# Smaller and earlier pieces of x and of the first weights in the opening of a hybrid decoder layer

## The chip, the cores and the metric

One core of one Trainium2 chip runs the whole program. The metric is the device time of one execution in microseconds, so lower is better. A run is repeated and the median is given.

## What is computed

One decoder layer for 256 prompt tokens and 8 sample tokens (264 columns side by side), in three residual sub-layers: attention and a state-space scan in parallel, cross-attention, and a convolutional feed-forward part. The change lies in the very first step, the input projection of the first sub-layer:

```python
def rms_norm(x, g):
    xf = x.astype(jnp.float32)
    y = xf * lax.rsqrt(jnp.mean(xf * xf, axis=-1, keepdims=True) + EPS)
    return (y * g.astype(jnp.float32)).astype(x.dtype)
...
    proj = rms_norm(x, w['g_mix']) @ w['w_in']
    q, k, v, z, xbc, dt_raw = jnp.split(proj, IN_SPLITS, axis=-1)
```

x has 2048 features, that is 16 blocks of 128; `w_in` has 2048 rows and 6688 columns, all in float32.

## The kernel before

Every operand of a product is split into a high part (rounded to a short float) and a low part (the rest), and a product is three matmuls: high weight by high x, high weight by low x, low weight by high x. The gain `g_mix` is multiplied into x while it is split; the norm's reciprocal root is applied after the product. The high parts are written by ScalarE (`x_hi` line 148, `w_hi` line 170), the low parts by VectorE (`x_lo` line 152, `w_lo` line 174); for the first pieces of weights VectorE also writes a high part (line 203).

The opening (lines 186 to 266) is written out by hand: the order in which SyncE, TensorE, ScalarE and VectorE issue their instructions is that of the code. It computes the first 512 columns of the projection in four PSUM banks, `first`, as two pairs p = 0 and 1 of 256 columns each. The loop of line 251 runs over the 16 blocks k of x, and for each block over the two pairs; `first_k` (line 237) issues six matmuls: for one pair, the three products one behind the other, each for two groups m of 128 columns. That is 12 matmuls for a block and 192 in all (line 243 in the trace). They are followed by 16 small float32 products for `dt` (line 249, 32 records in the trace), which multiply x by `wdt`, and by one product that sums the squares of x (line 266). That needs `acc0`, which comes from four squares on ScalarE (line 257) and five sums on VectorE (lines 258 to 263), ordered behind the splits.

Ahead of the first product four float32 matmuls on zeros (line 195) keep TensorE at work while the first data are on the way.

The loads: `load_x(k, n)` (line 142) brings n blocks of x, 132 KB each, by SyncE's queue; `w_load(p, k, n)` (line 160) brings n blocks of pair p, 128 KB each, by SyncE's queue or by ScalarE's. Blocks 0 and 1 come singly, blocks 2 to 7 in pieces of two, blocks 8 to 15 as x in pieces of two and weights in pieces of four. The raw weights of four blocks of a pair share one buffer of the tag `wraw` (line 163), of which there are four, so the raw weights of blocks 8 to 15 take the buffers of blocks 0 to 7 and their transfers are issued once the splits there are done. The high and low weights have four buffers of the same size each (`whi`, `wlo`), and a buffer is free once the products that read it are done.

The tag `B` holds four tiles of 8 by 264 columns. In the opening the two tiles `sw` for the squares take two of them (line 185); `t8`, `cpast`, `kv`, `kcT`, `vc` and `zz` follow. Behind the opening the order of the instructions is that of a planner that goes by modelled times; there `weights` (line 72) loads further weights in parts of 512 KB (line 79) into the same four `wraw` buffers and splits them (lines 85 and 86), and `proj` (line 104) multiplies them. The next pairs of the projection wait in their queues for the sum of line 266 and what goes with it (line 354).

Of the kernel before, what the change touches and what calls it, by code (L numbers as in the profile page):

```python
# [8 lines left out]
F32R = mybir.dt.float32r  # L9
# [6 lines left out]
KB = D // 128  # L16
TP, TS = 256, 8
T = TP + TS
# [29 lines left out]
def hybrid_decoder_step_kernel(ctx: ExitStack, tc: tile.TileContext, I, O):  # L48
    nc = tc.nc
    V, S, P, PE = nc.vector, nc.scalar, nc.gpsimd, nc.tensor  # L50

    cpool = ctx.enter_context(tc.tile_pool(name="cpool", bufs=1))
    wpool = ctx.enter_context(tc.tile_pool(name="wpool", bufs=2))
    apool = ctx.enter_context(tc.tile_pool(name="apool", bufs=1))
# [5 lines left out]
    def psum(tag):  # L60
        return ps.tile([128, 512], F32, tag=tag, name=tag, bufs=banks[tag])

    def T3(pool, n, dt=F32, tag=None, name=None, bufs=None):
        return pool.tile([128, n, T], dt, tag=tag, name=name or tag, bufs=bufs)


    NPART, WBUFS = 1024, 4

    def raw_part(n=NPART):
        return wpool.tile([128, n], F32, tag="wraw", name="wraw", bufs=4)  # L70
# [64 lines left out]
    wdt = T3(apool, 8, F32, "C", "wdt").rearrange("p a t -> p (a t)")[:, 0:512].rearrange("p (k c) -> p k c", c=32)  # L135
    w_in = I["w_in"]
    small = ctx.enter_context(tc.tile_pool(name="small", bufs=2))
    A = []
# [3 lines left out]
    def load_x(k, n):  # L142
        nc.sync.dma_start(out=xT[k // 4][:, k % 4:k % 4 + n, :], in_=I["xT"][:, k:k + n, :])

    def x_of(k):
        return xT[k // 4][:, k % 4, :], par[:, k:k + 1]

    def x_hi(k):
        x, g = x_of(k)
        return S.activation(out=A[k // 8][0][:, k % 8, :], in_=x, func=AF.Copy, scale=g)  # L150

    def x_lo(k):
        x, g = x_of(k)
        return V.scalar_tensor_tensor(out=A[k // 8][1][:, k % 8, :], in0=x, scalar=g, in1=A[k // 8][0][:, k % 8, :].bitcast(F32),
                                      op0=ALU.mult, op1=ALU.subtract)


    pre = {}

    def w_load(p, k, n, on=nc.sync):  # L160

        if k % 4 == 0:
            pre[p, k // 4] = (raw_part(), *(wpool.tile([128, NPART], F32R, tag=t, name=t, bufs=WBUFS) for t in ("whi", "wlo")))
        c = 256 * (k % 4)
        on.dma_start(out=pre[p, k // 4][0][:, c:c + 256 * n], in_=w_in[2 * p + k // 8][:, 256 * (k % 8):256 * (k % 8 + n)])

    def w_piece(p, k, n):
        return (w[:, 256 * (k % 4):256 * (k % 4 + n)] for w in pre[p, k // 4])

    def w_hi(p, k, n):  # L170
        raw, hi, _ = w_piece(p, k, n)
        return S.copy(out=hi, in_=raw)

    def w_lo(p, k, n):
        raw, hi, lo = w_piece(p, k, n)
        return V.tensor_tensor(out=lo, in0=raw, in1=hi.bitcast(F32), op=ALU.subtract)


    acc0 = small.tile([128, T], F32, tag="acc", bufs=1, name="acc0")
    table = small.tile([128, 1], F32, tag="r", bufs=2, name="table")  # L180
    first = [psum(t) for t in ("t", "t", "mm", "s")]
    warm = psum("x")
# [2 lines left out]
    sw = [T3(apool, 8, tag="B", name=f"sw{i}", bufs=4) for i in range(2)]  # L185
    with tc.manual_schedule(engines={mybir.EngineType.SP, mybir.EngineType.PE, mybir.EngineType.Activation, mybir.EngineType.DVE}):
        V.memset(acc0, 0.0)
        load_x(0, 1)
        S.dma_start(out=par[:, 0:16], in_=I["par"][:, 0:16])
        w_load(0, 0, 1, S)  # L190
        w_load(1, 0, 1, S)

        S.activation(out=table, in_=acc0[:, 0:1], func=AF.Copy)
        for _ in range(4):
            PE.matmul(warm[:, :T], acc0[:, 0:128], acc0, start=True, stop=True)
        for k, n in ((1, 1), (2, 2), (4, 2), (6, 2)):
            load_x(k, n)
            for p in range(2):
                w_load(p, k, n)
        for k in (0, 1):  # L200
            x_hi(k)
            raw, hi, _ = w_piece(0, k, 1)
            V.tensor_copy(out=hi, in_=raw)
            w_hi(1, k, 1)
            x_lo(k)
            for p in range(2):
                w_lo(p, k, 1)
        for k in (2, 4, 6):
            x_hi(k)
            w_hi(0, k, 2)  # L210
            w_hi(1, k, 2)
            x_hi(k + 1)
            x_lo(k)
            w_lo(0, k, 2)
            w_lo(1, k, 2)
            x_lo(k + 1)
        for k in (8, 12):
            load_x(k, 2)
            w_load(0, k, 4)
            w_load(1, k, 4)  # L220
            load_x(k + 2, 2)
        nc.sync.dma_start(out=wdt, in_=I["w_dt"])
        for k in (8, 12):
            for i in range(4):
                x_hi(k + i)
                x_lo(k + i)
                if i == 1:
                    w_hi(0, k, 4)
                    w_lo(0, k, 4)
            w_hi(1, k, 4)  # L230
            w_lo(1, k, 4)
        V.tensor_tensor(out=wdt, in0=wdt, in1=par[:, 0:16].unsqueeze(2).broadcast_to([128, KB, 32]), op=ALU.mult)
        nc.sync.dma_start(out=cst, in_=I["cst"])
        nc.sync.dma_start(out=par[:, 16:], in_=I["par"][:, 16:])
        nc.sync.dma_start(out=hcol, in_=I["hcol"])

        def first_k(p, k):
            wh, wl = (w.rearrange("p (k c) -> p k c", c=256)[:, k % 4, :] for w in pre[p, k // 4][1:])
            xh, xl = (a[:, k % 8, :] for a in A[k // 8])

            for i, (w, x) in enumerate(((wh, xh), (wh, xl), (wl, xh))):
                for m in range(2):
                    PE.matmul(first[2 * p + m][:, :T], w[:, m * 128:(m + 1) * 128], x, start=k + i == 0, stop=k == KB - 1 and i == 2)  # L243

        def dt_round(r):

            for j in range(4):
                k = 4 * r + j
                PE.matmul(dt_ps[32 * j:32 * j + 32, :T], wdt[:, k, :], xT[k // 4][:, k % 4, :], start=r == 0, stop=r == 3)

        for k in range(KB):
            for p in range(2):
                first_k(p, k)

        for i in range(2):
            for j in range(2):
                S.activation(out=sw[i][:, 4 * j:4 * j + 4, :], in_=xT[2 * i + j], func=AF.Square)
            V.tensor_tensor(out=sw[i][:, 0:4, :], in0=sw[i][:, 0:4, :], in1=sw[i][:, 4:8, :], op=ALU.add)

        sq_last = S.activation(out=table, in_=sw[1][:, 7, 0:1], func=AF.Sqrt)  # L260
        V.tensor_tensor(out=sw[0][:, 0:4, :], in0=sw[0][:, 0:4, :], in1=sw[1][:, 0:4, :], op=ALU.add)
        V.tensor_tensor(out=sw[0][:, 0:2, :], in0=sw[0][:, 0:2, :], in1=sw[0][:, 2:4, :], op=ALU.add)
        add_last = V.tensor_tensor(out=acc0, in0=sw[0][:, 0, :], in1=sw[0][:, 1, :], op=ALU.add)
        for r in range(4):
            dt_round(r)
        sum_last = PE.matmul(sum0[:, :T], cst[:, C_ONE:C_ONE + 128], acc0, start=True, stop=True)
# [157 lines left out]
    p = psum("y")  # L424
# [38 lines left out]
    p = psum("x")  # L463
# [5 lines left out]
    p = psum("x")  # L469
# [236 lines left out]
    for c in range(2):  # L706
        p = psum("x")
# [4 lines left out]
    for w, XT in enumerate((BT, CT)):  # L712
        p = psum("x")
# [71 lines left out]
    p = psum("x")  # L785
# [361 lines left out]
    p = psum("y")  # L1147
# [43 lines left out]
    for pi, (wh, wl) in enumerate(weights(I["w_co"][0])):  # L1191
        wh, wl = (w.rearrange("p (k c) -> p k c", c=512) for w in (wh, wl))
# [9 lines left out]
    for u in range(1, 4):  # L1202
        proj([I["w_co"][u]], [(OH, OL)], lambda m, pm, u=u: x2_ev(4 * u + m, pm), nb=4,
             tag=[cyc[(4 * (u - 1) + m) % 5] for m in range(4)])
# [255 lines left out]
def build(shapes):  # L1460

    import concourse.bacc as bacc

    nc = bacc.Bacc("TRN2", target_bir_lowering=False, num_devices=1)
    ins = {n: nc.dram_tensor(f"in_{n}_dram", s, dt, kind="ExternalInput").ap() for n, (s, dt) in shapes.items()}
    outs = {n: nc.dram_tensor(f"out_{n}_dram", s, F32, kind="ExternalOutput").ap() for n, s in _OUTS}
    with tile.TileContext(nc, schedule_with_timeline_sim=True) as tc:
        hybrid_decoder_step_kernel(tc, ins, outs)
    return nc
# [10 lines left out]
```

## Time and profile before

| | us |
|---|---|
| median of 3 runs | 1408.84 (1408.30 to 1409.17) |
| the profiled execution, its time | 1409.05 |
| the profiled execution, its span | 1407.2 |
| time outside the span (1409.05 - 1407.2) | 1.85 |
| TensorE busy in the span | 1399.3 |
| first product of line 243 starts | 5.07 |
| small products of line 249 start | 32.06 |

Times in the trace count from the start of the span. A row of a timeline has its start, its length, the engine, the line, the operation and the operands; neighbours of the same kind are merged ("x2"). The brackets hold the idle time of that engine just before the row, and what ended it. SPq and ACTq are queues that issue transfers; their rows are the issue, not the transfer. Matmuls overlap, so the distance between two starts tells what one costs, not its length.

### The profile page before, as it was taken

Reading aid. Unit: us, or ns where it says so; the run is one execution under the profiler, and the core shown is the slowest. Engines: PE = TensorE matmul, PEld = TensorE weight load, DVE = VectorE, ACT = ScalarE, POOL = GpSimd, SP = SyncE. Lnnn points to the kernel's source line nnn. Section 1 sums busy time; section 2 is a strip of 40 time slices with the busy share of each in tenths; the row PEclk is TensorE's granted clock in tenths of the full one; section 3 lists DMA queues with packets and bytes.
Section 4 is the critical chain, followed back from the end, with each engine's and each line's share of the span. In section 5 each row is a group of like instructions: output and inputs, shape, how many; then the busy total and the mean of one; then the engine's idle time right before and its main releaser. Section 6 shows DMA issues by size and latency. Waiting matters only on the chain.

```text
span 1407.2 us, 29055 instructions
## 1 busy us (share of the span) xinstructions
PE 1399.3 (99%) x11525; PEld 1367.5 (97%) x11525; DVE 1048.6 (75%) x1912; ACT 763.9 (54%) x1258; POOL 94.2 (7%) x282
## 2 busy tenths in 40 slices
PE   9999999999999999999999999999999999999999
PEld 8998899999999999899999999999999999999999
DVE  7969879999987784478777775777577757765664
ACT  7557765656545554566565553555355535543432
POOL 0000001211000000020010010001000100000000
PEclk9999999999999999999999999999999999999999
DMA  7963357777776567665566775676566656656564
GB/s 274 329 182 130 125 176 246 224 249 258 235 235 231 185 222 253 239 233 192 179 235 235 238 229 184 210 244 227 180 210 231 204 183 199 196 176 189 183 190 140
DMA packets 91207, 298.33 MB, mean 212 GB/s; under 512 B 12352, under 2 KB 18112, under 8 KB 90560
## 3 DMA queue, kind: packets, MB, share of 16 engines
q1 hardware_dynamic: 85136, 277.34, 59.9%
q0 software_dynamic: 5504, 18.88, 4.2%
q8 instruction: 90, 1.47, 0.4%
q14 instruction: 45, 0.37, 0.1%
q10 hardware_dynamic: 432, 0.27, 0.1%
HBM read 280.77 MB, written 16.23 MB: 211 GB/s over the span
## 4 chain that ended last, share of the span: by engine, by line
PE 98%; DMA 1%; DVE 0%; ACT 0%; issue 0%; SPq 0%
PE mm L100 21%; PE mm L101 21%; PE mm L102 21%; PE t L101 10%; PE t L100 10%; PE t L102 10%; PE s L523 1%; PE t L283 1%; PE y L757 1%; PE t L552 1%; DMA xT<-in_xT_dram 0%; PE y L773 0%; DMA wraw<-in_w_in_dram 0%; PE t L243 0%; PE x L283 0%; PE x L1052 0%
## 5 line engine op out<-in xcount | busy, mean ns | idle before, releaser
L85 ACT CAST whi<-wraw 128x1024 fp32r<-128x1024 f32 x440 | 460.3, 1048 | 526.8 <-PE mm L101 274.8
L86 DVE TENSOR_TENSOR wlo<-wraw,whi 128x1024 fp32r<-128x1024 f32 x440 | 539.8, 1228 | 232.7 <-ACT whi L85 230.3
L100 PE MATMUL mm<-x2h,whi 128*128 128x264 f32 x704 | 199.8, 284 | 0.0
L101 PE MATMUL t<-x2l,whi 128*128 128x264 f32 x704 | 199.8, 284 | 0.0
L100 PE MATMUL t<-x2h,whi 128*128 128x264 f32 x704 | 199.7, 284 | 0.0
L101 PE MATMUL mm<-x2l,whi 128*128 128x264 f32 x704 | 199.5, 283 | 0.0
L102 PE MATMUL t<-x2h,wlo 128*128 128x264 f32 x704 | 199.5, 283 | 0.0
L102 PE MATMUL mm<-x2h,wlo 128*128 128x264 f32 x704 | 199.3, 283 | 0.0
L101 PE MATMUL mm<-hl,whi 128*128 128x264 f32 x704 | 198.7, 283 | 0.0
L102 PE MATMUL mm<-hh,wlo 128*128 128x264 f32 x704 | 198.2, 283 | 0.0
L100 PE MATMUL mm<-hh,whi 128*128 128x264 f32 x704 | 197.2, 284 | 0.0
L100 PE MATMUL mm<-xh,whi 128*128 128x264 f32 x576 | 167.1, 292 | 0.0
L101 PE MATMUL mm<-xl,whi 128*128 128x264 f32 x576 | 164.3, 287 | 0.0
L102 PE MATMUL mm<-xh,wlo 128*128 128x264 f32 x576 | 162.9, 288 | 0.0
L101 PEld LDWEIGHTS t<-x2l,whi 128*128 128x128 f32 x704 | 132.6, 188 | 0.0
L101 PEld LDWEIGHTS mm<-x2l,whi 128*128 128x128 f32 x704 | 132.5, 188 | 0.0
L101 PEld LDWEIGHTS mm<-hl,whi 128*128 128x128 f32 x704 | 132.5, 188 | 0.0
L100 PEld LDWEIGHTS t<-x2h,whi 128*128 128x128 f32 x704 | 132.4, 188 | 0.0
L100 PEld LDWEIGHTS mm<-x2h,whi 128*128 128x128 f32 x704 | 132.4, 188 | 0.0
L102 PEld LDWEIGHTS t<-x2h,wlo 128*128 128x128 f32 x704 | 132.2, 188 | 0.0
L102 PEld LDWEIGHTS mm<-x2h,wlo 128*128 128x128 f32 x704 | 132.1, 188 | 0.0
L102 PEld LDWEIGHTS mm<-hh,wlo 128*128 128x128 f32 x704 | 132.0, 188 | 0.0
(474 smaller groups left out, 2948.4 us busy)
## 6 DMA issues: line engine op xcount, KB each, us to landing
wraw<-in_w_up_dram SPq DMA_DIRECT2D x176, 512.0 KB, 4.2
wraw<-in_w_in_dram SPq DMA_DIRECT2D x100, 512.0 KB, 4.8
wraw<-in_w_dn_dram SPq DMA_DIRECT2D x88, 512.0 KB, 4.3
wraw<-in_w_out_dram SPq DMA_DIRECT2D x48, 512.0 KB, 4.6
h<-in_h_dram POOLq DMA_DIRECT2D x32, 256.0 KB, 4.5
hn<-in_h_dram SPq DMA_DIRECT2D x16, 512.0 KB, 5.0
out_state_s_dram<-hn POOLq DMA_DIRECT2D x16, 512.0 KB, 3.7
e<-dram_la SPq DMA_DIRECT2D x16, 256.0 KB, 4.7
```

What stands on the lines that cost most here:

```text
L85: S.copy(out=hi, in_=x)
L86: V.tensor_tensor(out=lo, in0=x, in1=hi.bitcast(F32), op=ALU.subtract)
L100: PE.matmul(out, wh, xh, start=start, stop=False)
L101: PE.matmul(out, wh, xl, start=False, stop=False)
L102: return PE.matmul(out, wl, xh, start=False, stop=stop)
L283: return PE.transpose(out, in_, cst[0:k, C_ID:C_ID + k])
L523: PE.matmul(s3, qT[:, j, c * 128:c * 128 + 128], kbd[:, pp, :, 0:nk], start=True, stop=True)
L552: PE.matmul(o[64 * h:64 * h + 64, 0:128], vn[:, kb, pp, 64 * h:64 * h + 64], pt[:, h * nb + kb, :], start=kb == 0, stop=kb == nb - 1)
L757: PE.matmul(y[o:o + 64, (h // 2) * 128:(h // 2) * 128 + 128], xdt[:, h, :], es[h // 4][:, h % 4, :], start=True, stop=True)
```

## The change

The opening's loads and splits are cut in pieces of two blocks from block 2 to block 15, for the weights too. Blocks 0 and 1 of x come in one transfer; the weights of blocks 0 and 1 still come singly, and the one of pair 0, block 0 is now the first transfer of ScalarE's queue, with the gains (`par`) behind it. The raw weights of blocks 8 to 15 get two tiles of their own in the tag `B` (`late`), so that they wait for no buffer. The filling matmuls ahead of the first product are 264, 264, 264 and 128 columns wide, where they were four times 264. The matmuls of a block are ordered anew: high weights by high x for both pairs, high weights by low x for both pairs, then low weights by high x for both; from block 2 on, the products with low weights come behind the products with high weights of two blocks. ScalarE and VectorE split both blocks of x first, and then the weights of both pairs. `wdt` is loaded as before behind the last weights.

```diff
     pre = {}
+    late = [T3(apool, 8, tag="B", name=f"late{i}", bufs=4).rearrange("p a t -> p (a t)") for i in range(2)]
 
     def w_load(p, k, n, on=nc.sync):
         if k % 4 == 0:
-            pre[p, k // 4] = (raw_part(), *(wpool.tile([128, NPART], F32R, tag=t, name=t, bufs=WBUFS) for t in ("whi", "wlo")))
+            raw = late[k // 4 - 2][:, NPART * p:NPART * p + NPART] if k >= 8 else raw_part()
+            pre[p, k // 4] = (raw, *(wpool.tile([128, NPART], F32R, tag=t, name=t, bufs=WBUFS) for t in ("whi", "wlo")))
...
-        load_x(0, 1)
+        load_x(0, 2)
+        w_load(0, 0, 1, S)
         S.dma_start(out=par[:, 0:16], in_=I["par"][:, 0:16])
-        w_load(0, 0, 1, S)
         w_load(1, 0, 1, S)
+        for p in range(2):
+            w_load(p, 1, 1)
 
         S.activation(out=table, in_=acc0[:, 0:1], func=AF.Copy)
-        for _ in range(4):
-            PE.matmul(warm[:, :T], acc0[:, 0:128], acc0, start=True, stop=True)
-        for k, n in ((1, 1), (2, 2), (4, 2), (6, 2)):
-            load_x(k, n)
+        for n in (T, T, T, 128):
+            PE.matmul(warm[:, :n], acc0[:, 0:128], acc0[:, 0:n], start=True, stop=True)
+        for k in range(2, KB, 2):
+            load_x(k, 2)
             for p in range(2):
-                w_load(p, k, n)
-        for k in (0, 1):
-            x_hi(k)
-            raw, hi, _ = w_piece(0, k, 1)
-            V.tensor_copy(out=hi, in_=raw)
-            w_hi(1, k, 1)
+                w_load(p, k, 2)
+        nc.sync.dma_start(out=wdt, in_=I["w_dt"])
+        x_hi(0)
+        raw, hi, _ = w_piece(0, 0, 1)
+        V.tensor_copy(out=hi, in_=raw)
+        w_hi(1, 0, 1)
+        x_hi(1)
+        w_hi(0, 1, 1)
+        w_hi(1, 1, 1)
+        for k in range(2):
             x_lo(k)
             for p in range(2):
                 w_lo(p, k, 1)
-        for k in (2, 4, 6):
-            x_hi(k)
-            w_hi(0, k, 2)
-            w_hi(1, k, 2)
-            x_hi(k + 1)
-            x_lo(k)
-            w_lo(0, k, 2)
-            w_lo(1, k, 2)
-            x_lo(k + 1)
-        for k in (8, 12):
-            load_x(k, 2)
-            w_load(0, k, 4)
-            w_load(1, k, 4)
-            load_x(k + 2, 2)
-        nc.sync.dma_start(out=wdt, in_=I["w_dt"])
-        for k in (8, 12):
-            for i in range(4):
+        for k in range(2, KB, 2):
+            for i in range(2):
                 x_hi(k + i)
                 x_lo(k + i)
-                if i == 1:
-                    w_hi(0, k, 4)
-                    w_lo(0, k, 4)
-            w_hi(1, k, 4)
-            w_lo(1, k, 4)
+            for p in range(2):
+                w_hi(p, k, 2)
+                w_lo(p, k, 2)
...
-        def first_k(p, k):
-            wh, wl = (w.rearrange("p (k c) -> p k c", c=256)[:, k % 4, :] for w in pre[p, k // 4][1:])
-            xh, xl = (a[:, k % 8, :] for a in A[k // 8])
-
-            for i, (w, x) in enumerate(((wh, xh), (wh, xl), (wl, xh))):
-                for m in range(2):
-                    PE.matmul(first[2 * p + m][:, :T], w[:, m * 128:(m + 1) * 128], x, start=k + i == 0, stop=k == KB - 1 and i == 2)
+        def first_k(k, i):
+
+            for x in range(2 - i):
+                for p in range(2):
+                    w = pre[p, k // 4][1 + i].rearrange("p (k c) -> p k c", c=256)[:, k % 4, :]
+                    for m in range(2):
+                        PE.matmul(first[2 * p + m][:, :T], w[:, m * 128:(m + 1) * 128], A[k // 8][x][:, k % 8, :],
+                                  start=k + i + x == 0, stop=k == KB - 1 and i == 1)
...
-        for k in range(KB):
-            for p in range(2):
-                first_k(p, k)
+        for ks in ((0,), (1,), *((k, k + 1) for k in range(2, KB, 2))):
+            for i in range(2):
+                for k in ks:
+                    first_k(k, i)
```

## Rows read from the trace of the kernel before

**Rows 1.** The page's busy time of the engines: us, share of the span, instructions.

```profile
PE 1399.3 (99%) x11525; PEld 1367.5 (97%) x11525; DVE 1048.6 (75%) x1912; ACT 763.9 (54%) x1258; POOL 94.2 (7%) x282
```

**Rows 2.** TensorE's waits from 34 us to the end: us in total, times, longest.

```profile
PE mm L101 <- DVE ohl L1139: 1.4, 1, 1.4
```

**Rows 3.** Timeline of TensorE in the opening.

```profile
1.20 3.74 PE L195 MATMUL x<-acc 128*128 128x264 f32 x8 [1.20 <-DVE eps L279]
5.07 0.48 PE L243 MATMUL t<-xh,whi 128*128 128x264 f32 x2
...
9.63 0.51 PE L243 MATMUL t<-xh,whi 128*128 128x264 f32 x2 [1.12 <-ACT whi L172]
...
14.41 0.41 PE L243 MATMUL t<-xh,whi 128*128 128x264 f32 x2
...
18.79 0.41 PE L243 MATMUL t<-xh,whi 128*128 128x264 f32 x2
...
20.12 0.39 PE L243 MATMUL mm<-xh,whi 128*128 128x264 f32 x1 [0.45 <-ACT whi L172]
...
21.38 0.39 PE L243 MATMUL mm<-xh,wlo 128*128 128x264 f32 x1 [0.50 <-DVE wlo L176]
...
21.73 0.41 PE L243 MATMUL t<-xh,whi 128*128 128x264 f32 x2
...
32.06 1.99 PE L249 MATMUL x<-xT,wdt 128*32 128x264 f32 x32
```

**Rows 4.** Timeline of ScalarE in the opening.

```profile
3.55 0.50 ACT L150 ACTIVATE xh<-xT,par 128x264 fp32r<-128x264 f32 x1
5.41 0.41 ACT L172 CAST whi<-wraw 128x256 fp32r<-128x256 f32 x1 [1.36 <-DMA wraw<-in_w_in_dram]
...
6.97 0.41 ACT L172 CAST whi<-wraw 128x256 fp32r<-128x256 f32 x1 [0.73 <-DMA wraw<-in_w_in_dram]
8.31 0.52 ACT L150 ACTIVATE xh<-xT,par 128x264 fp32r<-128x264 f32 x1 [0.94 <-DMA xT<-in_xT_dram]
8.96 1.21 ACT L172 CAST whi<-wraw 128x512 fp32r<-128x512 f32 x2
10.07 0.92 ACT L150 ACTIVATE xh<-xT,par 128x264 fp32r<-128x264 f32 x2
...
12.08 0.92 ACT L150 ACTIVATE xh<-xT,par 128x264 fp32r<-128x264 f32 x2
...
24.59 4.00 ACT L257 ACTIVATE sw<-xT 128x1056 f32<-128x1056 f32 x4
```

**Rows 5.** Timeline of VectorE in the opening.

```profile
4.62 0.29 DVE L203 CAST whi<-wraw 128x256 fp32r<-128x256 f32 x1 [3.47 <-DMA wraw<-in_w_in_dram]
...
10.82 0.89 DVE L154 SCALAR_TENSOR_TENSOR xl<-xT,par,xh 128x264 fp32r<-128x264 f32 x2
...
12.83 0.89 DVE L154 SCALAR_TENSOR_TENSOR xl<-xT,par,xh 128x264 fp32r<-128x264 f32 x2
...
31.97 0.43 DVE L263 TENSOR_TENSOR acc<-sw 128x264 f32<-128x264 f32 x1
```

**Rows 6.** Timeline of SyncE's queue in the opening.

```profile
2.60 0.43 SPq L143 DMA_DIRECT2D xT<-in_xT_dram  x1
3.16 0.82 SPq L165 DMA_DIRECT2D wraw<-in_w_in_dram  x2
...
10.33 0.93 SPq L165 DMA_DIRECT2D wraw<-in_w_in_dram  x2
```

**Rows 7.** What SyncE's queue waited for, 0 to 20 us: total, times, longest.

```profile
SPq L165 <- DVE wlo L176: 2.6, 4, 1.5
```

**Rows 8.** Stretches of 1 us: length, busy time (instructions) by engine, clock, DMA share, GB/s.

```profile
5.00:6.00 1.00, 0.93 (x6) 0.88 (x7) 0.81 (x3) 0.59 (x2) 0.00 (x0) 1.00 1.07 224
...
9.00:10.00 1.00, 0.37 (x3) 0.37 (x4) 0.75 (x2) 1.00 (x2) 0.00 (x0) 1.00 1.06 403
```

**Rows 9.** Transfers issued from 2.4 to 3.0 us: KB each, median us to landing.

```profile
xT<-in_xT_dram SPq DMA_DIRECT2D x1, 264.0 KB, 5.7
```

## The prediction

> **What bounds the kernel now.** I read the page's busy times first: TensorE is busy for 1399.3 of 1407.2 us [rows 1], so the time can only fall by what TensorE waits, about 8 us in all. The list of its waits behind 34 us has one entry of note, 1.4 us [rows 2]; the other waits lie in the first 32 us and behind the last product. Whatever moves the end of the opening moves the rest of TensorE's work with it, one for one, as long as no new wait comes up there.
>
> In the opening the timeline of TensorE [rows 3] shows what a block costs with nothing late: from block 5 at 14.41 to block 8 at 18.79 are three blocks in 4.38 us, 1.46 us each; from block 9 at 21.73 to the small products at 32.06 are seven in 10.33 us, 1.48 us each. I take 1.47 us for 12 products, 0.122 us for one. Sixteen blocks would need 23.5 us; they take 32.06 - 5.07 = 27.0 us. So 3.5 us are lost, and that is the ceiling of this change unless the first product itself comes sooner. Where: blocks 0 and 1 take 9.63 - 5.07 = 4.56 us in place of 2.94 (1.6 lost, most of it the 1.12 us idle ahead of 9.63); block 8 takes 21.73 - 18.79 = 2.94 in place of 1.47 (1.5 lost, with idle times of 0.45 and 0.50 and slow starts around them); some 0.3 lie in blocks 2 to 4.
>
> What stands behind the two places. At 9.63 TensorE waits for the high weights of pair 0, blocks 2 and 3, which ScalarE starts at 8.96 after the x of block 2, for which it had waited until 8.31 [rows 4]. At 20.12 and 21.38 it waits for pieces of four blocks, whose transfers SyncE's queue could issue only once VectorE had finished with the raw buffers: the first at 10.33 [rows 6], with 2.6 us of such waits in all [rows 7].
>
> **The change part by part.**
>
> *Own raw tiles and pieces of two for blocks 8 to 15.* The waits of rows 7 go away, since nothing holds the `late` tiles before. Then three engines must each keep up with TensorE's 2.94 us for two blocks. ScalarE does a round of two blocks from 10.07 to 12.08, 2.01 us [rows 4]; VectorE from 10.82 to 12.83, 2.01 us [rows 5]; the transfers of two blocks are 264 + 2 x 256 KB, 811,000 bytes, and at the 403 GB/s of the stretch from 9 to 10 us [rows 8] take 2.0 us. All are faster by 0.9 us per round, so a lead once won grows, and the 1.5 us at block 8 go to nothing. More transfers are issued (24 on this queue for 21), at 0.43 us each on a queue that then has 2.0 us for three of them: covered, and if that cover went, the lead of the later rounds would pay first.
>
> *The first two blocks.* One issue of x goes away ahead of everything else on SyncE's queue, so x of blocks 2 and 3, issued at 2.60 before, is issued about 0.46 us earlier, at 2.14 [rows 6]. But the first product now needs 264 KB of x where 132 KB did. The weights of pair 0 landed at 4.62 [rows 5] and are issued one place earlier. I take 4.2 to 4.7 us for both and a first product at 4.8 to 5.3 us, no gain. Then the new order asks for the high weights of pair 1 after two products; those landed at 5.41 before [rows 4], and ScalarE does them behind `x_hi(0)`, so TensorE waits until about 5.8. ScalarE goes on with `x_hi(1)` and both weights of block 1; the last landed at 6.97 before [rows 4], is split at 7.4, and ten products later, at 8.6, block 1 is done: as before. What is lost in here costs nothing as long as it is less than the wait that follows.
>
> *Blocks 2 and 3.* This is the term that decides. Call L the landing of their x: 8.31 before [rows 4], that is 2.60 plus 5.7 us [rows 9]. Before, TensorE started at L + 1.32 = 9.63, because ScalarE did one block of x and then the weights of pair 0. Now ScalarE does both blocks of x (0.92 us), then the weights of both pairs (1.21 us) before the first four products can be through: the products of pair 1 start at S = L + 0.92 + 1.21 + 0.07 = L + 2.2. That is a new wait of 0.9 us which the change brings; VectorE's low parts come in the shadow of the 16 products with high weights (16 x 0.122 = 1.95 us against 2.01 for its round, which starts about 1.2 us earlier). L itself: with the earlier issue and the same 5.7 us it is 7.85. As a lower end: the stretch of single-block pieces moves 224 GB/s, the one of two-block pieces 403 [rows 8]; 270,000 bytes of x at the one or the other differ by 0.5 us, so L = 7.35. As an upper end for the whole term: the second weights of this piece (3.16 + 0.43 = 3.6 at issue before, rows 6) may be issued only when the larger first x has landed, 4.4 at the latest; with 5.7 us to landing and 0.62 us for the split (half of 1.21), S = 10.7 to 10.9. I take L = 7.85, S = 10.05, since only the issue moves for certain; the ends are S = 9.55 and 10.9.
>
> *The sum.* Behind S come 22 of the 24 products of blocks 2 and 3 (2.7 us) and twelve blocks (12 x 1.47 = 17.6 us): the small products start at 10.05 + 20.3 = 30.4 where they started at 32.06. Gain 1.7 us; with the ends of S, 2.2 and 0.85 us.
>
> *What is late next.* Squares and sums: ScalarE finishes its splits at S + 6 x 2.01 = 22.1 where the squares began at 24.59 [rows 4], so `acc0`, ready at 31.97 + 0.43 = 32.4 [rows 5], comes 2.5 us earlier at 29.9; TensorE asks for it behind the small products at 30.4 + 1.9 = 32.3. Covered by 2.4 us; were the squares to stay where they are, it would still be there at 32.4. High and low buffers: `w_hi(0, 8)` waits for blocks 0 to 3 (done at S + 2.7, asked for at S + 4.9), `w_hi(0, 12)` for blocks 4 to 7 (S + 8.6 against S + 9.0): covered, and behind a wait there would stand only ScalarE's later rounds, by then 3 us ahead. The tag `B`: `late` is read until about 22, and the tiles that follow are first needed by work behind the sum. The other products keep their number and shape: nothing.
>
> The profiled execution took 1409.05, 0.21 over the median of 1408.84. Its own sum is 1409.05 - 1.7 = 1407.35; against the median 1407.1.
>
> [...]
>
> **The rivals.**
>
> *The pieces land well ahead (gain 2.4 to 3.5 us, 1405.3 to 1406.4).* If fewer and longer transfers run at 403 GB/s from the start, L falls below 7.35 and the wait ahead of block 2 shrinks to some 0.5 us. For it: the slow stretch [rows 8]. Against it: the single weights of blocks 0 and 1 stay, and ScalarE's longer chain of 2.2 us stays.
>
> *The wait of block 8 goes, the one at block 2 grows (gain 0 to 0.85 us, 1408.0 to 1408.8).* S = 10.9 to 11.7, because x of blocks 2 and 3 doesn't land earlier (L = 8.31 alone gives S = 10.5 and a gain of 1.2) and the weights of pair 1 are issued late. For it: the order puts four splits ahead of the products of pair 1. Against it: one issue fewer ahead.
>
> [...]
>
> *The planner orders the rest differently.* The code behind the opening is the same, but its order goes by modelled times, and these move. What can be won is the 1.4 us of rows 2; what can be lost is about as much per new wait. 1405.7 to 1410, either sign.
>
> **How the numbers follow.** Forecast (1406.5 to 1408.0): 0.63. Early landing: 0.10. Wait at block 2 instead: 0.17. Clock: 0.04. Planner: 0.06, half each way. About 0.2% (2.8 us) is what a measurement of this kernel can tell from no change: faster than 1406.0 is most of the early case's lower half and a third of the planner's, 0.07; slower than 1411.7 is half of the clock's and a part of the planner's, 0.04; the rest, 0.89, is within. The range of 1405.7 to 1408.6 leaves out part of the early case (0.05), the clock (0.04), part of the planner (0.04) and the tail of the third case (0.04).
>
> **What would show it.** In the timeline of TensorE: a wait from about 8.6 to 10 that ends by the high weights of pair 1 and no wait of over 0.2 us from there to the small products, which start at 30.4. In SyncE's waits: no entry of `wlo` ahead of `wdt`. In ScalarE's: x of blocks 2 and 3 at about 7.85. Behind the opening: all rows 1.7 us earlier, the same 1.4 us wait. Wrong it would be if the first wait ended after 10.9, if rounds of two took any engine over 2.9 us, if products came 0.24 us apart, or if a wait of a microsecond stood behind 34 us that was not there before.

## The result: slower by a quarter of a per cent

The changed kernel takes 1411.32 us (median of 12 runs, 1410.60 to 1412.95), the kernel before 1408.05 us in the same comparison (12 runs, 1407.03 to 1409.17). The ratio is 1.0023, with a 95% interval of 1.0016 to 1.0031: 3.3 us slower, where a gain of 1.7 us (1407.1 us) was forecast, and outside the range of 1405.7 to 1408.6.

| | before | changed |
|---|---|---|
| median, us | 1408.05 | 1411.32 |
| the profiled execution, its time | 1409.05 | 1411.77 |
| its span | 1407.2 | 1409.8 |
| TensorE busy | 1399.3 | 1399.2 |
| first product of the projection starts | 5.07 | 5.84 |
| small products for dt start | 32.06 | 32.00 |
| product for the sum of squares starts | 33.98 | 35.85 |

TensorE's busy time is the same, so all of the loss is waiting. The small products start as before; of the 2.6 us by which the span is longer, 1.9 come up ahead of the product for the sum and 0.7 behind it, where a wait of 0.78 us for weights split at line 85 is new (at 346 us). TensorE's timeline in the changed kernel (start, length, engine, line, operation, operands, count, and in brackets the idle time before it and what ended it):

```profile
5.84 0.51 PE L235 MATMUL t<-xh,whi 128*128 128x264 f32 x2 [1.42 <-ACT xh L150]
...
8.97 0.40 PE L235 MATMUL t<-xh,whi 128*128 128x264 f32 x2
9.37 0.39 PE L235 MATMUL mm<-xh,whi 128*128 128x264 f32 x1
...
18.37 0.51 PE L235 MATMUL t<-xh,whi 128*128 128x264 f32 x2 [0.22 <-ACT whi L175]
...
24.70 0.41 PE L235 MATMUL t<-xh,whi 128*128 128x264 f32 x2
26.21 0.39 PE L235 MATMUL mm<-xh,whi 128*128 128x264 f32 x1 [1.10 <-ACT whi L175]
...
32.00 1.99 PE L242 MATMUL x<-xT,wdt 128*32 128x264 f32 x32
35.85 0.71 PE L261 MATMUL y<-acc,cst 128*128 128x264 f32 x2 [1.85 <-DVE acc L258]
```

Read it against [rows 3]. Blocks 2 and 3 start at 8.97, with pair 1 at 9.37: 0.7 us earlier than the 10.05 of the forecast for pair 1. At 18.37 block 8 starts, 0.4 us ahead of the kernel before. Then two waits come up that the forecast did not have: at block 12 the second pair starts 1.5 us behind the first (24.70 to 26.21, where it is 0.25 us at 12.14), and the sum waits 1.85 us for `acc0`, which the forecast had 2.4 us ahead of its need.

ScalarE, at the same places:

```profile
5.28 0.51 ACT L150 ACTIVATE xh<-xT,par 128x264 fp32r<-128x264 f32 x1 [1.63 <-DMA par<-in_par_dram]
...
7.08 0.92 ACT L150 ACTIVATE xh<-xT,par 128x264 fp32r<-128x264 f32 x2
...
17.70 1.26 ACT L175 CAST whi<-late 128x512 fp32r<-128x512 f32 x2 [2.29 <-DMA late<-in_w_in_dram]
...
25.54 0.62 ACT L175 CAST whi<-late 128x512 fp32r<-128x512 f32 x1 [1.25 <-DMA late<-in_w_in_dram]
...
27.98 4.00 ACT L252 ACTIVATE sw<-xT 128x1056 f32<-128x1056 f32 x4
```

Up to block 7 it runs ahead (x of block 2 is there at 7.08, forecast 7.85). Then it waits for the weights of the `late` tiles, 2.29 us at block 8, and ends its splits at 28.0 where the forecast had 22.1. The squares start at 27.98 instead of 24.59 [rows 4], and with them the sum. Why the weights are late stands in SyncE's queue:

```profile
8.32 0.43 SPq L143 DMA_DIRECT2D xT<-in_xT_dram  x1
9.50 0.93 SPq L79 DMA_DIRECT2D wraw<-in_w_in_dram  x2
10.49 1.13 SPq L168 DMA_DIRECT2D late<-in_w_in_dram  x2
...
15.74 0.33 SPq L79 DMA_DIRECT2D wraw<-in_w_in_dram  x1
16.95 0.33 SPq L168 DMA_DIRECT2D late<-in_w_in_dram  x1
17.66 0.33 SPq L79 DMA_DIRECT2D wraw<-in_w_in_dram  x1
18.25 1.11 SPq L168 DMA_DIRECT2D late<-in_w_in_dram  x1
```

Line 79 is the load in `weights`, of the later pairs of the projection, which are first used behind the sum. Four of these loads, 512 KB each, now stand among the opening's own: two between x of block 8 and the weights of block 8, one ahead of each of the two pieces of block 12. In the kernel before, the first of them was issued at 19.54, behind all of the opening:

```profile
19.54 17.75 SPq L79 DMA_DIRECT2D wraw<-in_w_in_dram  x8
```

They became possible because blocks 8 to 15 no longer take the four `wraw` buffers: two of these come free when VectorE ends its splits of blocks 2 and 3, at about 10 us, the other two behind blocks 6 and 7, at about 15 us. The planner, which puts what is outside the opening's written order wherever a queue and a buffer allow it (`weights` has high priority), filled them. 2.1 MB at the 406 GB/s of the stretch from 12 to 18 us are 5.2 us ahead of weights that TensorE needs next.

The first theory, then, is the queue (Q). The rivals were the first pieces and the order of splits (F: the first product comes at 5.84, 0.77 us later, because the gains `par` land at 5.28, behind the first weights on ScalarE's queue) and the planner's order behind the opening (R).

### The profile page after: what moved, and what is told of

Read it like the earlier page. It is cut to its first block, busy times and chain, and to the rows that moved or that the text cites. A ratio compares the mean times of both kernels' runs of the same rounds, so it can differ in the third digit from the quotient of the medians.

```text
span 1409.8 us, 29072 instructions
## 1 busy us (share of the span) xinstructions
PE 1399.2 (99%) x11525; PEld 1367.4 (97%) x11525; DVE 1049.9 (74%) x1915; ACT 766.2 (54%) x1263; POOL 93.4 (7%) x282
## 4 chain that ended last, share of the span: by engine, by line
PE 96%; DMA 2%; ACT 1%; DVE 0%; issue 0%; SPq 0%; ACTq 0%
PE mm L100 21%; PE mm L101 21%; PE mm L102 21%; PE t L101 9%; PE t L100 9%; PE t L102 9%; DMA late<-in_w_in_dram 1%; PE s L518 1%; PE t L278 1%; DMA wraw<-in_w_in_dram 1%; PE y L752 1%; PE t L547 1%; PE y L768 0%; DMA e<-dram_la 0%; PE x L278 0%; PE x L1047 0%
```

## The experiments

Each ratio is to the kernel before, run beside it on the same chip: its median was 1408.12 us beside e1 to e4, 1407.86 beside e5 to e8, and 1408.23 beside e9 to e12, which ran on another chip than e1 to e8. An "edge" is an order between two instructions that the code asks for.

| run | what | median, us | ratio to before (95%) |
|---|---|---|---|
| (changed kernel) | | 1411.32 | 1.0023 (1.0016 to 1.0031) |
| e1_hold | later loads held back | 1407.75 | 1.0001 (0.9992 to 1.0009) |
| e2_hold_par_first | and the gains first | 1409.41 | 1.0009 (1.0000 to 1.0018) |
| e3_before_late_tiles | before, own raw tiles alone | 1413.78 | 1.0042 (1.0029 to 1.0054) |
| e4_pieces_in_wraw | changed, without own tiles | 1408.08 | 1.0001 (0.9992 to 1.0010) |
| e5_hold_fill5 | e1 with more filling | 1407.68 | 0.9998 (0.9989 to 1.0007) |
| e6_half_ahead_fill5 | e5, two loads ahead | 1408.99 | 1.0007 (0.9998 to 1.0015) |
| e7_all_ahead_fill5 | e5, four loads ahead | 1411.64 | 1.0028 (1.0017 to 1.0039) |
| e8_before_short_fill | before, shorter filling alone | 1407.88 | 1.0001 (0.9993 to 1.0010) |
| e9_before_again | before, one more profile | 1408.33 | one run |
| e10_before_late_held | e3, later loads held back | 1407.94 | 1.0000 (0.9991 to 1.0009) |
| e11_before_two_held | e10 in pieces of two | 1407.48 | 0.9994 (0.9985 to 1.0003) |
| e12_hold_par_fill5 | e2 with more filling | 1407.71 | 0.9998 (0.9989 to 1.0006) |

### e1_hold: the changed kernel with the later loads held behind the opening

```diff
-        nc.sync.dma_start(out=hcol, in_=I["hcol"])
+        load_last = nc.sync.dma_start(out=hcol, in_=I["hcol"])
...
-            with tc.issue_after(sum_last.ins), tc.issue_after(add_last.ins), tc.issue_after(sq_last.ins):
+            with tc.issue_after(sum_last.ins), tc.issue_after(add_last.ins), tc.issue_after(sq_last.ins), tc.issue_after(load_last.ins):
```

> The changed kernel, with one edge more: the loads of the third and later pairs of weights may be issued on SyncE's queue only behind the opening's last load (hcol). Theory Q (queue): the loss is that four loads of 512 KB of later weights, which the planner put between the opening's loads because the wraw buffers had come free, hold up the weights of blocks 8 to 13 by 2 MB / 400 GB/s = 5 us of transfer. It expects no wait for late weights over 0.3 us, the small products at 29.9 to 30.5 us where the changed kernel has 32.00, the sum without a wait, and 1405.5 to 1407 us, 1 to 2.5 us faster than the kernel before. Theory F (first pieces): the loss is the first product at 5.84 where it was 5.07 and the order of splits; it expects 1410 to 1411, as the changed kernel. Theory R (rest): the planner's order behind the opening is what costs; it expects an opening as in Q, but a time over 1409.

Measured: 1407.75 us, 3.6 us below the changed kernel and level with the kernel before. One edge takes the whole loss away. SyncE's queue, ScalarE and TensorE in its trace:

```profile
15.78 1.01 SPq L168 DMA_DIRECT2D late<-in_w_in_dram  x2
...
19.79 3.19 SPq L79 DMA_DIRECT2D wraw<-in_w_in_dram  x4
```

```profile
23.22 4.00 ACT L252 ACTIVATE sw<-xT 128x1056 f32<-128x1056 f32 x4
```

```profile
5.84 0.81 PE L235 MATMUL t<-xh,whi 128*128 128x264 f32 x2 [1.21 <-ACT xh L150]
...
6.89 0.65 PE L235 MATMUL t<-xl,whi 128*128 128x264 f32 x2
...
7.77 0.65 PE L235 MATMUL t<-xh,wlo 128*128 128x264 f32 x2
...
31.54 1.99 PE L242 MATMUL x<-xT,wdt 128*32 128x264 f32 x32
33.46 0.71 PE L261 MATMUL y<-acc,cst 128*128 128x264 f32 x2
```

The last piece of weights is issued at 15.78, the squares start at 23.22, and no wait is left in the opening but the one ahead of the first product. Theories F and R fall as causes of the loss: both expected this kernel over 1409. Yet the gain that Q expected (1405.5 to 1407) isn't there either. The trace shows one reason that the expectation didn't have: from 6.89 to 7.77 four products pass in 0.88 us, 0.22 each, where they take 0.122 later. This pace lasts until about 10.5. In e3 below products come 0.22 us apart where the granted clock reads 0.50; so I take the distance here for that lower level of the clock too. This is a guess, since the granted clock reads 1.00 here, from 5 to 10 us and from 10 to 15. The runs spread from 1406.52 to 1409.93, wider than those of the kernel before beside them (1406.92 to 1408.83).

### e3_before_late_tiles and e10_before_late_held: own raw tiles alone

The kernel before with the two lines of the change that make the `late` tiles, and nothing else; e10 has the edge of e1 on top.

```diff
+    late = [T3(apool, 8, tag="B", name=f"late{i}", bufs=4).rearrange("p a t -> p (a t)") for i in range(2)]
...
-            pre[p, k // 4] = (raw_part(), *(...))
+            raw = late[k // 4 - 2][:, NPART * p:NPART * p + NPART] if k >= 8 else raw_part()
+            pre[p, k // 4] = (raw, *(...))
```

> The kernel before with one part of the change alone: the raw weights of blocks 8 to 15 in tiles of their own. In its queue the planner then puts one load of 512 KB ahead of x of block 8, one behind it, and two behind the weights of block 12. Theory Q: slower than before: the weights of block 8 land about 2.6 us later than they would, those of block 8 at about 18 us, less what the freed buffers give (their issue at 10.33 waited for splits); small products at 32.5 to 35 where before has 32.06, time 1408.5 to 1412. Theory F: the first blocks are those of before, so nothing of the loss is here: at or below the kernel before, 1406 to 1408.

Measured: 1413.78 us, 5.7 us over the kernel before, more than the whole change loses. The planner put four loads of 512 KB in here as well (one ahead of x of block 8, one behind it, two around the last x). The first waits are as expected; then the granted clock falls, to which the prediction gave a chance of 0.04. Stretches of 2 us in its trace (length, TensorE busy with the count, granted clock, transfer share, GB/s):

```profile
18.00:20.00 2.00, 0.49 (x4) 1.00 1.01 395
20.00:22.00 2.00, 0.97 (x6) 1.00 1.03 422
22.00:24.00 2.00, 0.87 (x4) 0.62 1.01 407
24.00:26.00 2.00, 1.99 (x9) 0.50 1.04 417
26.00:28.00 2.00, 2.00 (x11) 0.50 0.89 350
28.00:30.00 2.00, 2.00 (x14) 0.67 0.14 49
30.00:32.00 2.00, 2.00 (x19) 1.00 0.00 0
```

```profile
25.00 0.64 PE L245 MATMUL t<-xh,whi 128*128 128x264 f32 x2
25.44 0.64 PE L245 MATMUL t<-xl,whi 128*128 128x264 f32 x2
...
37.27 1.10 PE L251 MATMUL x<-xT,wdt 128*32 128x264 f32 x16
```

TensorE is busy for 2.3 of 6 us from 18 to 24, with three waits of 1.5, 0.5 and 1.65 us at block 8, and the granted clock reads 0.62, 0.50, 0.50 and 0.67 in the four stretches from 22 to 30 before it is back at 1.00 in the stretch from 30. From 24 to 28 TensorE does 20 matmuls, from 30 to 32 alone 19; at 0.50 two products take 0.44 us (25.00 to 25.44). The seven blocks behind block 8 take 12.3 us (25.00 to 37.27), where they took 10.3 before: about 1.9 us of the 5.7 are the clock's, by an estimate from 20 products (25.00 to 29.37) at 0.22 us in place of 0.122; the rest is for the most part waits for late weights. The time is 1.8 us over the range expected, which had waits alone.

> e3_before_late_tiles with the loads of later weights held behind the opening's last load: the kernel before with own raw tiles for blocks 8 to 15 and nothing else. Theory Q: all that e3 lost comes back (5 us), and the stall at block 8 goes: no wait of TensorE over 0.3 us from block 4 on, small products at 29.5 to 30.5, 1406.5 to 1407.5. If own tiles cost by themselves (their place in the tag B), it stays over 1409.

Measured: 1407.94 us. All of e3's loss comes back with the edge, so the tiles as such (their place in the tag `B` included) cost nothing that shows (the interval is 0.1% either way). The gain that was expected didn't come: the stall at block 8 is down to one wait of 0.50 us for the low weights of four blocks, but in this execution x of block 2 landed at 8.39 and the small products started at 31.63.

### e4_pieces_in_wraw: the changed kernel without own tiles

```diff
-            raw = late[k // 4 - 2][:, NPART * p:NPART * p + NPART] if k >= 8 else raw_part()
+            raw = raw_part()
```

> The changed kernel without its own raw tiles: the raw weights of blocks 8 to 15 take the wraw buffers again, in pieces of two blocks; no later weights stand between the opening's loads then. Theory Q: a piece of block 8 waits for the splits of blocks 2 and 3 (done at about 10) only for its first issue, so block 8 is ready by 18.5 at the latest; small products at 30 to 31.5, time 1406 to 1408, no slower than before. Theory F: as slow as the changed kernel, 1410 to 1411.5.

Measured: 1408.08 us, no slower than before: with the buffers occupied by the opening's own pieces no later load fits in between. The first of them is issued behind all of the opening:

```profile
20.61 15.04 SPq L79 DMA_DIRECT2D wraw<-in_w_in_dram  x8
```

Theory F expected 1410 to 1411.5 and falls a second time. Theory Q is a little off too: the time is just over its 1406 to 1408, and the small products start at 31.82, not by 31.5.

### e5, e6, e7: the dose

In all three the filling ahead of the first product is five matmuls of 264 columns, meant to let the clock disturb less:

```diff
-        for n in (T, T, T, 128):
+        for n in (T,) * 5:
```

e5 holds all later loads as e1 does, e6 lets the first two of them go ahead, e7 all four, as in the changed kernel. The line of e6, in `weights` (`loads["last"]` is the load of `hcol`; e7 has no edge on it at all):

```diff
-                nc.sync.dma_start(out=x, in_=src[:, o:o + w])
+                loads["n"] += 1
+                with tc.issue_after(loads["last"]) if loads["n"] > 2 and "last" in loads else ExitStack():
+                    nc.sync.dma_start(out=x, in_=src[:, o:o + w])
```

Theory C starts from e1's trace, where the first 22 products or so came 0.22 us apart and later ones 0.122. It is a guess that takes this distance for the lower level of the clock, the granted 0.50 of e3, and the shorter filling for its cause.

> e1_hold with five filling matmuls of 264 columns ahead of the first product in place of 264, 264, 264 and 128. [...] Theory C (clock): the shorter filling and the wait behind it let the first products run at the lower level in many executions; with TensorE at work until the first product they run at 0.122, the small products start at 29.3 to 30.2 and the time is 1405.5 to 1406.7, 1 to 2 us below e1_hold, with a narrower spread. Theory L (landings): the spread of e1_hold is one of the transfers, and the filling changes nothing: 1407 to 1408.5.

> As e5_hold_fill5, but the first two of the four loads of later weights stand again between x of block 8 and the weights of block 8, as in the changed kernel; the other two are held back. Theory Q (queue): 1 MB at 400 GB/s = 2.6 us later weights from block 8 on; the lead there takes part of it, so 1 to 2 us above e5_hold_fill5 and the sum waits less than 1 us. A theory by which only the number of queued transfers counts, not their bytes, expects no difference to e5_hold_fill5.

> The changed kernel with five filling matmuls: all four loads of later weights ahead. Theory Q: 3 to 4.5 us above e5_hold_fill5, that is 1409 to 1411, and at or up to 1.5 us below the changed kernel, since the clock can't win back what waits for data; the small products wait for weights of block 12 and the sum for acc0 as in the changed kernel. Theory C alone (all of the loss is the clock): as e5_hold_fill5.

Measured: 1407.68, 1408.99 and 1411.64 us, that is 0, 1.3 and 4.0 us for 0, 1.05 and 2.1 MB ahead. The squares' start on ScalarE and the sum's on TensorE, from the three traces in this order (the lines of e6 are shifted by 4 or 5):

```profile
22.41 4.01 ACT L252 ACTIVATE sw<-xT 128x1056 f32<-128x1056 f32 x4
```

```profile
25.38 4.00 ACT L257 ACTIVATE sw<-xT 128x1056 f32<-128x1056 f32 x4
```

```profile
28.20 4.01 ACT L252 ACTIVATE sw<-xT 128x1056 f32<-128x1056 f32 x4
```

```profile
29.91 1.99 PE L242 MATMUL x<-xT,wdt 128*32 128x264 f32 x32
31.83 0.71 PE L261 MATMUL y<-acc,cst 128*128 128x264 f32 x2
```

```profile
33.24 0.71 PE L266 MATMUL y<-acc,cst 128*128 128x264 f32 x2 [0.90 <-DVE acc L263]
```

```profile
36.06 0.71 PE L261 MATMUL y<-acc,cst 128*128 128x264 f32 x2 [1.85 <-DVE acc L258]
```

The splits end 3.0 and 5.8 us later, about the bytes ahead divided by 400 GB/s (2.6 and 5.2): the delay passes to ScalarE in full. TensorE takes up what its lead allows, and the sum starts 1.4 and 4.2 us later, as the medians do. So it is the loads ahead in the queue. The theory of the number of transfers, as put down for e6, expected no difference to e5 and falls; bytes and number grow together in these three, though. What tells them apart is e11 against e10 (below): four transfers more for the same bytes (and the splits in another order), and the squares start at 23.16 against 24.86, no later. e7 is a small miss: it was put at 1409 to 1411 and not above the changed kernel, and is 0.3 us above it.

Theory C came out half right at most. In e5 the products come 0.12 us apart from 6.26 on, the small products start at 29.91, close to the 30.4 of the forecast, and the spread narrows (1406.90 to 1408.67). But the median didn't move, and that the filling did it isn't shown: the changed kernel, with the shorter filling, has 0.12 us from 6.43 on, and e6 and e7, with five matmuls, only from 7.0.

### e8_before_short_fill and e9_before_again: what the base was

e8 is the kernel before with the fourth filling matmul 128 columns wide; e9 is the kernel before, profiled once more.

```diff
-        for _ in range(4):
-            PE.matmul(warm[:, :T], acc0[:, 0:128], acc0, start=True, stop=True)
+        for n in (T, T, T, 128):
+            PE.matmul(warm[:, :n], acc0[:, 0:128], acc0[:, 0:n], start=True, stop=True)
```

> The kernel before with one part of the change alone: the fourth filling matmul is 128 columns wide. TensorE then ends its filling at about 4.4 to 4.6 us in place of 4.94, and the first product stays at 5.07. Theory C: the first products run 0.22 us apart in some or most executions: 0.5 to 1.5 us slower, wider spread. Theory L: no change.

> The kernel before, unchanged, profiled once more. In its recorded trace x of block 2 landed at 8.31 and the small products started at 32.06; in e8_before_short_fill, whose transfers are the same, x of block 2 landed at 7.23 and the small products started near 30.6. If the recorded trace was a late one among the executions (theory B: the base of the sum was 1 us too high), this one has x of block 2 at 7.2 to 7.8, a wait ahead of block 2 under 0.8 us, and small products at 30.5 to 31.5. If landings are the same in each execution, it shows 8.3, 1.1 and 32.06 again.

Measured: e8 1407.88 us, no change, although its first six products ran 0.22 us apart or more: the wait ahead of block 2 took that in. e9 took 1408.33 us. Their timelines of TensorE, e8 first:

```profile
8.94 0.51 PE L243 MATMUL t<-xh,whi 128*128 128x264 f32 x2 [0.23 <-ACT whi L172]
...
30.65 1.99 PE L249 MATMUL x<-xT,wdt 128*32 128x264 f32 x32
```

```profile
9.37 0.51 PE L243 MATMUL t<-xh,whi 128*128 128x264 f32 x2
...
31.71 1.99 PE L249 MATMUL x<-xT,wdt 128*32 128x264 f32 x32
```

With the same transfers in the same order, x of block 2 was there at 8.31 in the trace of [rows 4], at 8.06 in e9 and at 7.23 in e8, and the small products started at 32.06, 31.71 and 30.65. The 1.12 us ahead of 9.63 in [rows 3] is 0.23 us in the one and gone in the other, in part because their slow first products ended later; block 2 itself started 0.7 and 0.3 us earlier. The recorded execution, 1409.05 us, lies near the upper end of the runs of its kernel. The medians bear theory B out, though e9 alone misses its numbers for x (8.06 where 7.2 to 7.8 was expected) and for the small products (31.71 where 30.5 to 31.5 was).

### e2 and e12: the gains first

e2 is e1 with the gains issued ahead of the first weights on ScalarE's queue, as in the kernel before; e12 has five filling matmuls on top.

```diff
-        w_load(0, 0, 1, S)
         S.dma_start(out=par[:, 0:16], in_=I["par"][:, 0:16])
+        w_load(0, 0, 1, S)
         w_load(1, 0, 1, S)
```

> As e1_hold, and the gains (par, 8 KB) are again issued ahead of the weights of pair 0, block 0 on ScalarE's queue, as in the kernel before. Theory Q: the gains land some 2 us earlier than 5.28, and the first product starts at 4.8 to 5.2 where the changed kernel has 5.84; blocks 2 and 3 then start when their weights are there, so the time is within 0.5 us of e1_hold, 0 to 0.5 faster. Theory F: faster than e1_hold by 0.8 us or more.

Before e12 was put on record, e2 had taken 1409.41 us where e1 took 1407.75, and in e2's trace the first 28 products or so had come 0.22 us apart, until 12.9 us.

> e2_hold_par_first with five filling matmuls of 264 columns. [...] Theory C: that is the clock, and with TensorE at work until the first product it goes: products at 0.122 us apart from 6 us on at the latest, 1407.0 to 1407.9, 1.5 us below e2. If it is the later landing of the weights of pair 1 (split at 6.54 in e2, at 5.74 in e1), the filling changes nothing: 1409 to 1410.

Measured: e2 1409.41 us, 1.7 us slower than e1 where 0 to 0.5 faster was expected, a miss. TensorE in its trace:

```profile
4.92 0.78 PE L235 MATMUL t<-xh,whi 128*128 128x264 f32 x2 [0.28 <-DVE whi L208]
...
7.00 0.59 PE L235 MATMUL mm<-xh,whi 128*128 128x264 f32 x1 [1.31 <-ACT whi L175]
7.61 0.64 PE L235 MATMUL t<-xl,whi 128*128 128x264 f32 x2
...
8.49 0.64 PE L235 MATMUL t<-xh,wlo 128*128 128x264 f32 x2
...
32.94 1.99 PE L242 MATMUL x<-xT,wdt 128*32 128x264 f32 x32
```

The first product does start at 4.92, but after two of them TensorE waits 1.3 us more for the weights of pair 1, and the products run 0.22 us apart until about 12.9. With more filling, e12, the median is 1407.71, 1.7 us below e2, as theory C said (e12 and e2 ran on two chips, on which the kernel before differs by 0.1 us). Its profiled execution, at 1409.54 the slowest of its eleven, does not show what theory C gave as the reason:

```profile
8.12 0.39 PE L235 MATMUL mm<-xh,whi 128*128 128x264 f32 x1 [1.86 <-ACT whi L175]
...
9.47 0.64 PE L235 MATMUL t<-xh,whi 128*128 128x264 f32 x2
```

TensorE waits 1.86 us at 8.12 in spite of the filling, the products run 0.22 us apart from 9.47 to about 12.6, the granted clock is 0.72 from 10 to 15 us, and the small products start at 32.98, no earlier than in e2. The gain is thus shown by the medians alone, and that it is the clock's is a guess, not shown.

### e11_before_two_held: the parts that might gain

The kernel before with own tiles, the edge of e1, pieces of two from block 2 to 15 and the splits in the order of blocks 2 to 7; first pieces, filling and products as before.

```diff
+        for k in range(2, KB, 2):
+            x_hi(k)
+            w_hi(0, k, 2)
+            w_hi(1, k, 2)
+            x_hi(k + 1)
+            x_lo(k)
+            w_lo(0, k, 2)
+            w_lo(1, k, 2)
+            x_lo(k + 1)
```

> e10 with the weights of blocks 8 to 15 in pieces of two and the splits of blocks 8 to 15 in the order of blocks 2 to 7; blocks 0 to 7, the filling and the order of products are those of the kernel before. Theory Q: as e10 within 0.5 us, since ScalarE, VectorE and the transfers each need 2.0 us for two blocks and TensorE 2.94: 1406.3 to 1407.5. Against e5_hold_fill5 (1407.68) it tells what the new first pieces and the new order of products are worth: if those gain, e11 is above e5; if they lose, below.

Measured: 1407.48 us, the lowest median of all, with no wait of 0.25 us or more left on TensorE between the first product and 600 us. Against the kernel before the ratio is 0.9994 (0.9985 to 1.0003), so a gain over it isn't shown; against the changed kernel it is 3.8 us. Nor does it differ from e5 by more than the spread, so what the new first pieces and the new order of products are worth stays open: less than can be measured here.

## Why the prediction was wrong

**The sign.** The step that failed is the one on own raw tiles: "The waits of rows 7 go away, since nothing holds the `late` tiles before". That held for the opening's own loads. It left out the other side of the same edit: the `wraw` buffers of blocks 0 to 7, which had been handed on to blocks 8 to 15, come free and have another taker on the same queue, the load of line 79. The prediction counted 24 transfers on the queue in place of 21 and 0.43 us for each; there were 28 in the stretch, and four of them carried 2.1 MB that nobody needed yet. That term was put at nothing; e1 against the changed kernel puts it at 3.6 us, e7 against e5 at 4.0. Of the signs of being wrong that the prediction named, the one for behind 34 us came: the wait at the sum ends at 35.85. (The bytes of a round are 795,000, 264 + 512 KB, and not 811,000; its 2.0 us at 403 GB/s stay.)

**The planner as a rival.** It was there, with a chance of 0.06, but placed behind the opening, where the trace shows waits. Its place was inside the opening: an order written by hand fixes the order among its own instructions and doesn't keep others out. The trace of before held a hint: up to 40 us the loads of line 79 waited 3.8 us there for VectorE's splits of the opening's raw buffers (line 176), so a buffer that came free had a taker.

**Covered by 2.4 us.** The sum's cover was worked out from ScalarE's rounds of 2.0 us with transfers in time. It was the first to go: the squares stand behind the splits, so all of the queue's 5 us arrived there, and 1.85 us of it on TensorE.

**Blocks 2 and 3.** The mechanism was right and the wait shorter than put: pair 1 started at 9.37 in place of 10.05, since x landed at 7.08 at the latest, under the lower end of the range (7.35). What ScalarE then waited for were the weights of pair 1 (0.19 us here, 0.50 in e5, 1.21 in e7), which the prediction had in its upper end alone. The first product was later than said, 5.84 in place of 4.8 to 5.3, because the gains moved one place back on ScalarE's queue (issued at 1.18 us and landed 4.0 later, where before had 0.74 and 2.4; with the gains first again, in e2, it starts at 4.92); I had moved the first weights forward and not asked what stood behind them. The weights themselves landed with x: both were issued at 0.74 and took 4.0 and 3.9 us. Before block 2 the later start cost nothing, as the prediction had said of this stretch.

**The gain of 1.7 us.** Without the later loads the opening ends about where the sum said: 29.91 in e5 and 31.54 in e1 with its slow first products, against 30.4. But the median gain is 0.2 to 0.4 us, within the intervals. One part is that the base was mis-sized: the profiled execution was taken as typical but for 0.21 us. Over 12 runs the median is 1408.05, 1.0 us below it and 0.8 below the 1408.84 of the sum; in e9 and e8 block 2 started 0.3 and 0.7 us earlier than in the recorded trace. The other part is that e5, with 1407.68, is still 0.6 us over the forecast of 1407.1. Its trace has 2.0 us outside the span where before had 1.85, and 1375.4 us from the start of the small products to the end where before had 1375.1; what costs that isn't shown.

**The clock.** The prediction gave it a chance of 0.04, half of it for a time over 1411.7, and named products 0.24 us apart as a sign. The cost of a slow product that this was worked out from, no run shows: in e1, e2 and e3 slow products came 0.22 us apart, 0.10 more than 0.122. In the changed kernel's own trace it didn't happen (0.12 us from 6.43 on, a granted clock of 1.00 in every stretch up to 36 us); in e1 and e2 the first products were slow, and in e3 the granted clock fell after waits. Around the one wait of 1.12 us in the kernel before it read 1.00 (each stretch of 1 us from 8 to 11, one of them in [rows 8]); in e3 it fell during three waits close together, to 0.62 from 22 to 24 us and to 0.50 behind them, and was back at 1.00 from 30 us on, with TensorE at work since 24. That a shorter filling costs time no trace here shows; the medians of e2 and e12 go that way with 1.7 us, those of e1 and e5 don't move.

## What to carry to other kernels

A buffer that an edit sets free is an offer to whoever else shares its pool: before costing "own tiles" at nothing, list who else allocates from the old ones, on which queue their loads stand and with what priority, and hold them back by an edge where the order matters. What stood ahead of a needed piece in the queue was paid for here at about the transfer rate: 2.1 MB, 5.2 us at 406 GB/s, put ScalarE's squares back by 5.8 us (e7 against e5), and TensorE's sum by 4.2, since its lead took up the rest. And a sum made against one profiled execution should first ask where that execution lies among the runs: x of block 2 landed at 8.31 us in one trace, and at 8.06 and 7.23 in two others of the same transfers.

## What the runs showed of the hardware that was not expected

- The pace of TensorE's first products differs between kernels and executions: they came 0.22 us apart until 10.5 us in e1, 12.9 in e2, 6.4 in e8 and 7.3 in e9, and 0.12 us from 6.1 to 6.4 us on in the recorded trace of before, in the changed kernel and in e5. The filling matmuls ended between 4.4 and 5.1 us, and the granted clock read 1.00 from 5 to 10 and from 10 to 15 us, in all of them.
- In e3, where waits left TensorE busy for 2.3 us between 18 and 24, the granted clock was 0.50 from 24 to 28 us and for a part of the stretches next to it, and 20 matmuls took 4 us where 19 took 2 later.
- The landing of the same transfer, issued at the same point of the same queue, moved by 1.1 us between executions (x of block 2: 7.23 in e8, 8.06 in e9, 8.31 in the recorded trace of before).
